# Some low parts of split operands made by adding transfers instead of VectorE subtractions

## The chip, the cores and the metric

The kernel runs on one core of a Trainium2 chip. The engines of the core have one in-order instruction stream each: TensorE (PE in the profile; its weight loads are PEld), VectorE (DVE), ScalarE (ACT), GpSimd (POOL) and SyncE (SP). SP, ACT and POOL can issue transfers (DMA). The metric is the device time of one execution in microseconds. The kernel before takes 1139.64 us, the median of three runs (1139.55 to 1140.3).

## The reference, cut to what matters

One layer of a streaming encoder on 512 tokens of width 1024, in float32:

```python
f = swiglu(rms_norm(h, ffn1_pre_g[l]), ffn1_w1[l], ffn1_w3[l], ffn1_w2[l])
h = h + 0.5 * rms_norm(f, ffn1_post_g[l])
u = rms_norm(h, mix_pre_g[l])
q, k, v, xr, xg = jnp.split(u @ w_in[l], splits, axis=-1)
xr = causal_conv(xr, conv_w[l], conv_b[l])
hr = rg_lru(xr, ...)                                   # a scan over the tokens
y_a = (hr * jax.nn.gelu(xg)) @ w_lru_out[l]
y_b = swa_sink_attention(q, k, v, attn_sinks[l], bias) @ w_attn_out[l]
g = jax.nn.sigmoid(u @ w_gate[l] + b_gate[l]).reshape(b, s, N_BRANCHES, d)
merged = g[:, :, 0] * y_a + g[:, :, 1] * y_b
h = h + rms_norm(merged @ w_o[l], mix_post_g[l])
f = swiglu(rms_norm(h, ffn2_pre_g[l]), ffn2_w1[l], ffn2_w3[l], ffn2_w2[l])
h = h + 0.5 * rms_norm(f, ffn2_post_g[l])
```

## The kernel before

**Split operands.** Every float32 operand x of a product is split into a high part (x rounded to the type `fp32r` by an ACT copy) and a low part (x minus the high part, a DVE subtraction). A product then takes three matmuls: high by high, low by high, high by low. `split2` (L192) makes both parts; weights get theirs in `split_to` (L152) or in `Pairs.prep` (L493). So each weight tile of 128x1024 (512 KB) costs one load by SP, one ACT copy (`whi`), one DVE subtraction (`wlo`) and its matmuls.

**The stages.** First FFN; its output product `tok_gemm`, which at the end leaves the normed activations transposed in `uT` (high and low part); then the mixer, around which this case turns; then the attention, the output projections and the second FFN. In the mixer PE runs in this order: the eight `xr` tiles, the eight gate tiles `wg` 0 to 7 (each a unit of 24 matmuls, `mm_feat` L197, with lines L204 to L206), the V product (L1113 to L1115, four token groups), the four pairs of `xg` tiles (`GeluPairs`, L621), then `wk`, `wq` and the attention.

**The xg pairs.** Two weight tiles (ra, rb) and two halves of the tokens are multiplied with seven instead of eight products of quarter blocks (a Strassen-Winograd scheme). On the weight side there are the sums S1 to S4 (`S12`, `S34`, made by POOL, L518 to L524), on the activation side T1 to T4 (keys `t1` to `t4` of `X3`). The seven products of pair n are groups of 12 matmuls (`mm_s`, L473 to L475), in the order a11, S1, (the a22 of pair n-1), S2, a12, S4, S3. ACT copies results between groups (L638, L640, L644, L656), because a later group goes on adding in the same bank. Step i of `prep(m, i)` makes the weights of pair m:

- i = 0: the sums S12 and S34, on POOL
- i = 1: high and low part of ra, which holds a11 and a12
- i = 2, 3: high and low part of S12 and of S34
- i = 4: high and low part of a22, a half of rb

During pair n the loop `run` calls prep(n+1, 1) after group S1, prep(n+1, 2) after S2, prep(n+1, 3) after S4, then prep(n+1, 4) and prep(n+2, 0). So the a11 of pair n+1 uses what prep(n+1, 1) made some five groups earlier, and S1 of pair n+1 what prep(n+1, 2) made. Pair 0 is prepared ahead, at the places in `PREP_AT`; `PREP_1` is the place of prep(1, 0).

**T1 to T4.** POOL makes them from copies `xf` of the transposed activations (L1066); `t_hi` copies the high part on ACT and `t_lo` subtracts on DVE. `T_AT` gives the places of both.

**What sets the order.** The text of the program is the order of each engine's instructions. `later(n, fn)` puts off work by n places, `point()` marks a place (two in each unit of 24 matmuls, one in each V group); a lower rank goes first. Instructions wait on semaphores for what they read, and for the last user of the slot which they write: all big tiles come from a pool of 42 slots, so a load by SP waits until a slot is free.

**Beside it.** The recurrent branch runs on ACT and DVE during the mixer. Its scans (L1047, a product, and L1048, the scan, eight of each, tiles `ig`) come at the last places (`SCAN_AT`), after ACT's square roots (L1044), and share DVE with the V parts (`V`, L195) and with the weights of the xg pairs.

Of the kernel before, what the change touches and what calls it, by code (L numbers as in the profile page):

```python
# [11 lines left out]
F32R = mybir.dt.float32r  # L12
AF = mybir.ActivationFunctionType
ALU = mybir.AluOpType

P = 128
SEQ = 512
D = 1024
# [33 lines left out]
def hybrid_layer(ctx: ExitStack, tc: tile.TileContext, a: dict, out: bass.AP):  # L52
    nc = tc.nc
    act, dve, pool, pe, sp = nc.scalar, nc.vector, nc.gpsimd, nc.tensor, nc.sync

    cp = ctx.enter_context(tc.tile_pool(name="cp", bufs=1))
    sm = ctx.enter_context(tc.tile_pool(name="sm", bufs=4))
    sb = ctx.enter_context(tc.tile_pool(name="sb", bufs=NSLOT))
    pp = ctx.enter_context(tc.tile_pool(name="pp", bufs=8, space=bass.MemoryType.PSUM))
# [3 lines left out]
    def slot(shape, dt=F32, name="s"):  # L63
        uid[0] += 1
        return sb.tile(shape, dt, tag="slot", name=f"{name}_{uid[0]}")
# [9 lines left out]
    def f32(ap):  # L75
        return ap.bitcast(F32)
# [25 lines left out]
    order = []  # L102
# [33 lines left out]
    raws, pairs = {}, {}  # L136
# [10 lines left out]
    def dma_to(n):  # L147
        while st["dma"] < min(n, len(order)):
            dma_one(st["dma"])
            st["dma"] += 1  # L150

    def split_to(n):  # L152
        while st["split"] < min(n, len(order)) and st["split"] not in paired:
            k = st["split"]
            dma_to(k + 1)
            r = raws.pop(k)
            hi = slot([P, D], F32R, name="whi")
            lo = slot([P, D], F32R, name="wlo")
            act.activation(hi, r, AF.Copy)
            dve.tensor_tensor(out=lo, in0=r, in1=f32(hi), op=ALU.subtract)  # L160
            pairs[k] = (hi, lo)
            st["split"] += 1

    def get(nm, i, ahead=2, rawahead=3):

        k = st["get"]
        assert order[k] == (nm, i), (order[k], nm, i)
        dma_to(k + 1 + ahead)
        split_to(k + 1 + ahead)
        dma_to(st["split"] + rawahead)  # L170
        st["get"] += 1
        return pairs.pop(k)
# [5 lines left out]
    def later(n, fn, rank=1):  # L178
        uid[0] += 1
        due.append((now[0] + n, rank, uid[0], fn))  # L180
# [11 lines left out]
    def split2(hi, lo, src):  # L192

        act.activation(hi, src, AF.Copy)  # L194
        dve.tensor_tensor(out=lo, in0=src, in1=f32(hi), op=ALU.subtract)  # L195
# [138 lines left out]
    def tok_gemm(nm, xs, n, R, gpost_name, scale, gpre_name, first, x_to=None, xf=None, spill=False, then=None, eps=None):  # L334
# [38 lines left out]
        us, trs = {}, {}  # L373
        ep = lambda t: D * EPS if eps is None else eps[:, t : t + 1]
        split_to(st["get"] + len(first))
        dma_to(st["split"] + 2)
        for t in range(NT):
# [48 lines left out]
    def get_ahead():  # L426
        split_to(st["get"] + 2)
        dma_to(st["split"] + 3)
# [49 lines left out]
    class Pairs:  # L478
# [14 lines left out]
        def prep(self, m, i, eng=None):  # L493
            if m >= len(self.jobs) or (m, i) in self.ready:
                return
            self.ready.add((m, i))
            k = self.k0 + 2 * m
            if i == 0:
                if k not in loaded or k + 1 not in loaded:
                    self.raws(m)  # L500
                s12, s34 = slot([P, 2 * QH], name="S12"), slot([P, 2 * QH], name="S34")
                self.w[m] = {"r": (raws.pop(k), raws.pop(k + 1)), "s": (s12, s34)}
            W = self.w[m]
            (ra, rb), (s12, s34) = W["r"], W["s"]
            a11, a12, a21, a22 = ra[:, :QH], ra[:, QH:], rb[:, :QH], rb[:, QH:]

            def both(src, w=2 * QH):
                hi = slot([P, w], F32R, name="whi")
                lo = slot([P, w], F32R, name="wlo")
                split2(hi, lo, src)  # L510
                return hi, lo

            def halves(p, a, b):
                W[a] = p[0][:, :QH], p[1][:, :QH]
                W[b] = p[0][:, QH:], p[1][:, QH:]

            def sums34(e):
                e.tensor_tensor(out=s34[:, QH:], in0=a12, in1=s12[:, QH:], op=ALU.subtract)  # L518
                e.tensor_tensor(out=s34[:, :QH], in0=a11, in1=a21, op=ALU.subtract)  # L519

            if i == 0:
                e = eng or pool
                e.tensor_tensor(out=s12[:, :QH], in0=a21, in1=a22, op=ALU.add)
                e.tensor_tensor(out=s12[:, QH:], in0=s12[:, :QH], in1=a11, op=ALU.subtract)  # L524
                if self.R is None:
                    sums34(e)
            elif i == 1:
                halves(both(ra), "a11", "a12")
            elif i == 2:
                if self.R is not None:  # L530
                    sums34(dve)
                halves(both(s12), "s1", "s2")
            elif i == 3:
                halves(both(s34), "s3", "s4")
            elif i == 4:
                t = slot([P, 2, QH], F32R, name="w22")
                split2(t[:, 0, :], t[:, 1, :], a22)
                W["a22"] = t[:, 0, :], t[:, 1, :]
            if all((m, x) in self.ready for x in range(5)):
                del W["r"], W["s"]  # L540
# [219 lines left out]
    xg, tg = {(hh, th): slot([P, 4, 256], name="xg") for hh in range(2) for th in range(2)}, {}  # L760
# [101 lines left out]
    def uview(hh, th):  # L862

        return lambda e, k: uT[:, e, 4 * hh + k, th * 256 : th * 256 + 256]

    def pair_view(p):
        return lambda e, k: p[e][:, k, :]
# [77 lines left out]
    for f in range(NG, NC1):  # L945
# [4 lines left out]
    bs = tok_gemm(  # L950
        "w2a", hid, FT, RF, "ffn1_post_g", 0.5, "mix_pre_g", [("xr", i) for i in range(4)], hid.to, xf=xf, spill=True, eps=veps)
    hid = None
# [100 lines left out]
    X3 = {"b11": uview(0, 0), "b21": uview(1, 0), "b22": uview(1, 1)}  # L1053
    pairs_g = GeluPairs(("xg",), 0, 8, X3)

    def t_hi(key, src):
        X3[key] = slot([P, 4, 256], F32R, name="Xh")
        act.activation(X3[key], src, AF.Copy)

    def t_lo(key, src):  # L1060
        hi, lo = X3[key], slot([P, 4, 256], F32R, name="Xl")
        dve.tensor_tensor(out=lo, in0=src, in1=f32(hi), op=ALU.subtract)
        X3[key] = pair_view((hi, lo))

    for o_, p_, q_ in (((0, 0), (0, 1), (0, 0)), ((0, 1), (1, 1), (0, 1)), ((1, 1), (1, 1), (0, 0)), ((1, 0), (1, 0), (1, 1))):
        pool.tensor_tensor(out=xf[o_], in0=xf[p_], in1=xf[q_], op=ALU.subtract)  # L1066
    for n, (key, o_) in enumerate((("t1", (0, 0)), ("t3", (0, 1)), ("t2", (1, 1)), ("t4", (1, 0)))):
        later(T_AT[0][n], lambda key=key, o_=o_: t_hi(key, xf[o_]), 3)
        later(T_AT[1][n], lambda key=key, o_=o_: t_lo(key, xf.pop(o_)), 3)
    for i, p in enumerate(PREP_AT):  # L1070
# [50 lines left out]
    X3 = pairs_g = None  # L1121
# [221 lines left out]
    X2 = pairs_b = None  # L1343
    tok_gemm("w2b", hid, FT, RF, "ffn2_post_g", 0.5, None, [], hid.to)

# [8 lines left out]
SCAN_AT = (25, 25, 25, 25, 26, 26, 26, 26)  # L1354
SCAN_LAG = (1, 1, 2, 2, 2, 2, 3, 5)

T_AT = (3, 4, 5, 6), (13, 15, 18, 20)
PREP_AT = (19, 21, 23, 24, 25)
PREP_1 = 24
NSLOT = 42  # L1360
RF = 7
RO = 6

# [58 lines left out]
```

## Time and profile before

| | |
|---|---|
| median of three runs | 1139.64 us (1139.55 to 1140.3) |
| the profiled execution | 1139.73 us, span 1137.9 us |
| PE | 1121.4 us busy, 99% of the span |
| DVE | 832.2 us, 73% |
| ACT | 617.9 us, 54% |
| POOL | 344.5 us, 30% |
| HBM | 116.50 MB read, 7.33 MB written |

Rows of the timeline read: start in us from the span's start, length in us, engine, line, operation, written tile<-read tiles, partitions x elements and type, count; in brackets the idle time of the engine before it, and what ended it. Rows of a grouping view read: line, engine, operation, tiles and shapes, count | busy us, mean ns of one | idle time before them, and what ended it. Rows of transfers read: written tile<-source, issuing queue, count, size of each, median us from issue to landing. `uT`, `Xh` and `Xl` are activations, `whi` and `wlo` weights (the page leaves out buffer numbers), `S` the weight sums, `raw_...` loaded weights.

### The profile page before, as it was taken

How to read it: one execution, taken by the hardware profiler on the slowest of the kernel's cores; microseconds unless marked ns; L12 is line 12 of the kernel's file. 1: busy time of each engine (PE TensorE's matmuls, PEld its weight loads, DVE VectorE, ACT ScalarE, POOL GpSimd, SP SyncE). 2: the span in 40 equal slices, each digit the busy share in tenths (PEclk: the TensorE clock that was granted, in tenths of full speed). 3: DMA queues.
4: the chain of work that ended last, by engine and by line, in shares of the span. 5: the costliest groups of instructions: out<-in, count | busy, mean ns of one | idle time of the engine just before them, and what ended most of it. 6: DMA issues, size and time to landing. Idle time of an engine off the chain costs nothing.

```text
span 1137.9 us, 17855 instructions
## 1 busy us (share of the span) xinstructions
PE 1121.4 (99%) x6973; PEld 1011.6 (89%) x6973; DVE 832.2 (73%) x1235; ACT 617.9 (54%) x1101; POOL 344.5 (30%) x263
## 2 busy tenths in 40 slices
PE   9999999999999999799999999999999999999997
PEld 7899999988889878798888888889999999998886
DVE  5889989796346989986678855767899777975313
ACT  7755555474236598466656653356555555574211
POOL 0043444200002302421456543000965566700000
PEclk9999999999999999899999999999999999999999
DMA  9226553365304112234133233531323332255101
GB/s 346 89 88 150 139 119 112 82 220 162 129 38 167 56 56 74 75 99 162 44 88 93 89 84 125 174 122 39 111 87 100 112 106 81 93 189 179 40 19 56
DMA packets 37139, 124.98 MB, mean 110 GB/s; under 512 B 4528, under 2 KB 6448, under 8 KB 37056
## 3 DMA queue, kind: packets, MB, share of 16 engines
q1 hardware_dynamic: 34128, 114.89, 31.0%
q0 software_dynamic: 2640, 8.43, 3.7%
q8 instruction: 55, 0.90, 0.3%
q10 hardware_dynamic: 288, 0.52, 0.1%
q14 instruction: 28, 0.23, 0.1%
HBM read 116.50 MB, written 7.33 MB: 109 GB/s over the span
## 4 chain that ended last, share of the span: by engine, by line
PE 96%; DVE 2%; ACT 0%; issue 0%; DMA 0%; DVEq 0%; SPq 0%
PE c L474 12%; PE c L473 12%; PE c L475 12%; PE f L204 10%; PE f L205 10%; PE f L206 9%; PE acc L222 8%; PE acc L223 8%; PE acc L224 8%; PE pt L1221 1%; DVE ig L1048 1%; DVE ig L1047 1%; PE s L1185 1%; PE s L1184 1%; PE tr L314 1%; PE o L1237 1%
## 5 line engine op out<-in xcount | busy, mean ns | idle before, releaser
L474 PE MATMUL c<-uT,wlo 128*128 128x256 f32 x504 | 143.3, 284 | 7.6 <-DVE wlo L195 7.6
L204 PE MATMUL f<-uT,whi 128*128 128x512 f32 (+1 forms) x408 | 146.7, 360 | 0.0
L205 PE MATMUL f<-uT,wlo 128*128 128x512 f32 (+1 forms) x408 | 145.3, 356 | 0.0
L206 PE MATMUL f<-uT,whi 128*128 128x512 f32 (+1 forms) x408 | 145.2, 356 | 0.0
L474 PE MATMUL c<-Xh,wlo 128*128 128x256 f32 x504 | 143.2, 284 | 0.0
L475 PE MATMUL c<-uT,whi 128*128 128x256 f32 x504 | 143.2, 284 | 0.0
L473 PE MATMUL c<-Xh,whi 128*128 128x256 f32 x504 | 143.1, 284 | 0.0
L473 PE MATMUL c<-uT,whi 128*128 128x256 f32 x504 | 143.0, 284 | 0.0
L475 PE MATMUL c<-Xl,whi 128*128 128x256 f32 x504 | 142.9, 284 | 0.0
L222 PE MATMUL acc<-whi,hT 128*128 128x512 f32 x352 | 137.1, 390 | 0.0
L223 PE MATMUL acc<-wlo,hT 128*128 128x512 f32 x352 | 137.0, 389 | 0.0
L224 PE MATMUL acc<-whi,hT 128*128 128x512 f32 x352 | 136.9, 389 | 0.0
L195 DVE TENSOR_TENSOR wlo<-S,whi 128x1024 fp32r<-128x1024 f32 x84 | 124.1, 1477 | 2.0 <-ACT whi L194 1.2
L474 PEld LDWEIGHTS c<-uT,wlo 128*128 128x128 f32 x504 | 97.3, 193 | 7.9 <-DVE wlo L195 7.8
L194 ACT ACTIVATE whi<-S 128x1024 fp32r<-128x1024 f32 x84 | 86.1, 1054 | 22.0 <-DVE S L519 22.0
L473 PEld LDWEIGHTS c<-Xh,whi 128*128 128x128 f32 x504 | 97.2, 193 | 0.4 <-issue 0.3
L474 PEld LDWEIGHTS c<-Xh,wlo 128*128 128x128 f32 x504 | 97.0, 192 | 0.4 <-DVE wlo L195 0.3
L475 PEld LDWEIGHTS c<-uT,whi 128*128 128x128 f32 x504 | 97.3, 193 | 0.0
L473 PEld LDWEIGHTS c<-uT,whi 128*128 128x128 f32 x504 | 97.2, 193 | 0.0
L475 PEld LDWEIGHTS c<-Xl,whi 128*128 128x128 f32 x504 | 97.0, 193 | 0.0
L204 PEld LDWEIGHTS f<-uT,whi 128*128 128x128 f32 x408 | 77.1, 189 | 12.1 <-issue 1.4
L206 PEld LDWEIGHTS f<-uT,whi 128*128 128x128 f32 x408 | 77.1, 189 | 11.0
(341 smaller groups left out, 2797.3 us busy)
## 6 DMA issues: line engine op xcount, KB each, us to landing
raw_w2a<-in_w2a_dram SPq DMA_DIRECT2D x22, 512.0 KB, 3.9
raw_w1b<-in_w1b_dram SPq DMA_DIRECT2D x22, 512.0 KB, 4.3
raw_w3b<-in_w3b_dram SPq DMA_DIRECT2D x22, 512.0 KB, 3.9
raw_w2b<-in_w2b_dram SPq DMA_DIRECT2D x22, 512.0 KB, 4.2
raw_w3a<-in_w3a_dram SPq DMA_DIRECT2D x21, 512.0 KB, 4.5
raw_w1a<-in_w1a_dram SPq DMA_DIRECT2D x20, 512.0 KB, 4.4
raw_wg<-in_wg_dram SPq DMA_DIRECT2D x16, 512.0 KB, 3.7
raw_xr<-in_xr_dram SPq DMA_DIRECT2D x8, 512.0 KB, 3.7
```

What stands on the lines that cost most here:

```text
L194: act.activation(hi, src, AF.Copy)
L195: dve.tensor_tensor(out=lo, in0=src, in1=f32(hi), op=ALU.subtract)
L204: pe.matmul(ps[:, c0:c1], wh[:, s], h_, start=k == 0, stop=False)
L205: pe.matmul(ps[:, c0:c1], wl[:, s], h_, start=False, stop=False)
L206: pe.matmul(ps[:, c0:c1], wh[:, s], l_, start=False, stop=k == KT - 1)
L222: pe.matmul(acc[n], x[:, 0, c], wh[:, s], start=first, stop=False)
L223: pe.matmul(acc[n], x[:, 0, c], wl[:, s], start=False, stop=False)
L224: pe.matmul(acc[n], x[:, 1, c], wh[:, s], start=False, stop=last)
L314: pe.transpose(ps[:, k * P : (k + 1) * P], hg[:, kk * P : (kk + 1) * P], ident)
L473: pe.matmul(ps, wh[:, s], xh, start=first, stop=False, skip_group_check=True)
L474: pe.matmul(ps, wl[:, s], xh, start=False, stop=False, skip_group_check=True)
L475: pe.matmul(ps, wh[:, s], xl, start=False, stop=k == 3, skip_group_check=True)
```

## The change

A new function makes a low part without DVE: ACT writes the negative of the high part (a copy with scale -1, rounded the same way) into the low part's slot, and a transfer issued by POOL then adds the original float32 values onto it, from where they lie (DRAM for weights, the slot for T1 to T4). Eleven low parts are made this way: T1 to T4, the gate tiles 0 to 3, and the ra of the xg pairs 1, 2 and 3 (not of pair 0). Each takes one DVE subtraction away and adds one ACT copy, one issue on POOL and 512 KB of transfer. The low parts of T1 to T4 are moved from the places 13, 15, 18, 20 to 4, 5, 6, 7, one place behind their high parts.

```diff
+    def split_dma(r, src, shape=(P, D), hi=None):
+
+        lo = slot(list(shape), F32R, name="wlo")
+        if hi is None:
+            hi = slot(list(shape), F32R, name="whi")
+            act.activation(hi, r, AF.Copy)
+        act.activation(lo, r, AF.Copy, scale=-1.0)
+        pool.dma_start(out=lo, in_=src, accum_op=ALU.add)
+        return hi, lo
...
     def split_to(n):
...
             r = raws.pop(k)
-            hi = slot([P, D], F32R, name="whi")
-            lo = slot([P, D], F32R, name="wlo")
-            act.activation(hi, r, AF.Copy)
-            dve.tensor_tensor(out=lo, in0=r, in1=f32(hi), op=ALU.subtract)
-            pairs[k] = (hi, lo)
+            if order[k] in BY_DMA:
+                nm, i = order[k]
+                pairs[k] = split_dma(r, a[nm][i * P : (i + 1) * P, :])
+            else:
+                hi = slot([P, D], F32R, name="whi")
+                lo = slot([P, D], F32R, name="wlo")
+                act.activation(hi, r, AF.Copy)
+                dve.tensor_tensor(out=lo, in0=r, in1=f32(hi), op=ALU.subtract)
+                pairs[k] = (hi, lo)
...
             elif i == 1:
-                halves(both(ra), "a11", "a12")
+                nm, t_ = order[k]
+                p = split_dma(ra, a[nm][t_ * P : (t_ + 1) * P, :]) if nm in BY_DMA and m else both(ra)
+                halves(p, "a11", "a12")
...
     def t_lo(key, src):
-        hi, lo = X3[key], slot([P, 4, 256], F32R, name="Xl")
-        dve.tensor_tensor(out=lo, in0=src, in1=f32(hi), op=ALU.subtract)
-        X3[key] = pair_view((hi, lo))
+        X3[key] = pair_view(split_dma(src, src, (P, 4, 256), X3[key]))
...
-T_AT = (3, 4, 5, 6), (13, 15, 18, 20)
+T_AT = (3, 4, 5, 6), (4, 5, 6, 7)
...
+BY_DMA = {("wg", i) for i in range(4)} | {"xg"}
```

## The prediction

> **What bounds the kernel now.** I read the page first, then the waits of TensorE, and only then the place where the one large wait stands.
>
> ```profile
> span 1137.9 us, 17855 instructions
> ...
> PE 1121.4 (99%) x6973; PEld 1011.6 (89%) x6973; DVE 832.2 (73%) x1235; ACT 617.9 (54%) x1101; POOL 344.5 (30%) x263
> ...
> PE 96%; DVE 2%; ACT 0%; issue 0%; DMA 0%; DVEq 0%; SPq 0%
> ```
> ```profile
> engine line waited for: us in total, times, longest us
> PE c L474 <- DVE wlo L195: 7.6, 1, 7.6
> ```
>
> TensorE (PE) is busy for 99% of the span, and the chain that ended last is PE but for 2% on DVE. PE's only large wait is 7.6 us, once, on a low part that DVE makes. So work taken off DVE is worth something only as far as it ends that wait sooner, and whatever makes PE wait anew costs its full length. The timeline of PE puts the wait in time; the rows are the first matmuls on either side and the starts of the groups that follow.
>
> ```profile
> 471.44 0.28 PE L473 MATMUL c<-uT,whi 128*128 128x256 f32 x1
> 479.34 0.58 PE L474 MATMUL c<-uT,wlo 128*128 128x256 f32 x1 [7.63 <-DVE wlo L195]
> ...
> 482.32 0.58 PE L474 MATMUL c<-Xh,wlo 128*128 128x256 f32 x1
> ...
> 485.78 0.39 PE L473 MATMUL c<-Xh,whi 128*128 128x256 f32 x1
> ...
> 491.76 0.28 PE L474 MATMUL c<-uT,wlo 128*128 128x256 f32 x1
> ...
> 501.84 0.28 PE L474 MATMUL c<-uT,wlo 128*128 128x256 f32 x1
> ```
>
> It is the second of the four x_gate pairs (n=1, counted from 0). At 471.44 its first matmul has the high part of a11; the second needs the low part and gets it at 479.34. At 482.32 the product with S1 waits once more, for the low part of S12. Pair 2 needs its first low part at 491.76, pair 3 at 501.84. What DVE did until then:
>
> ```profile
> 459.07 0.42 DVE L195 TENSOR_TENSOR V<-v,V 128x256 fp32r<-128x256 f32 x1 [2.18 <-ACT V L194]
> 459.41 1.83 DVE L1047 TENSOR_TENSOR ig<-xc_t,ig 128x512 f32<-128x512 f32 x1
> ...
> 462.41 0.67 DVE L1047 TENSOR_TENSOR ig<-xc_t,ig 128x512 f32<-128x512 f32 x1
> ...
> 469.30 2.20 DVE L1048 TENSOR_TENSOR_SCAN ig<-xc_t,ig 128x512 f32<-128x512 f32 x1
> ...
> 473.14 2.17 DVE L1048 TENSOR_TENSOR_SCAN ig<-xc_t,ig 128x512 f32<-128x512 f32 x1
> 475.23 1.68 DVE L1047 TENSOR_TENSOR ig<-xc_t,ig 128x512 f32<-128x512 f32 x1
> ...
> 478.09 1.20 DVE L195 TENSOR_TENSOR wlo<-raw_xg,whi 128x1024 fp32r<-128x1024 f32 x1
> 479.20 0.68 DVE L1047 TENSOR_TENSOR ig<-xc_t,ig 128x512 f32<-128x512 f32 x1
> 479.92 1.22 DVE L1048 TENSOR_TENSOR_SCAN ig<-xc_t,ig 128x512 f32<-128x512 f32 x1
> 481.06 1.20 DVE L195 TENSOR_TENSOR wlo<-S,whi 128x1024 fp32r<-128x1024 f32 x1
> ...
> 482.51 0.41 DVE L650 TENSOR_TENSOR cc<-c,ct 128x256 f32<-128x256 f32 x1
> ```
>
> From 459.07 DVE runs through the V parts and eight products and scans, then the two low parts that PE needs. The row at 459.07 decides most of this case: before it DVE had been idle for 2.18 us. It was not behind; it waited for ACT.
>
> ```profile
> 404.53 1.06 ACT L159 ACTIVATE whi<-raw_wg 128x1024 fp32r<-128x1024 f32 x1
> ...
> 409.27 1.05 ACT L159 ACTIVATE whi<-raw_wg 128x1024 fp32r<-128x1024 f32 x1
> ...
> 454.36 0.38 ACT L194 ACTIVATE V<-v 128x256 fp32r<-128x256 f32 x1 [2.09 <-PE v L1115]
> ...
> 466.16 1.05 ACT L194 ACTIVATE whi<-raw_xg 128x1024 fp32r<-128x1024 f32 x1
> ...
> 483.01 1.28 ACT L630 ACT_TABLE_LOAD   x1 [10.99 <-DVE cc L650]
> ...
> 485.36 0.37 ACT L638 ACTIVATE ct<-c 128x256 f32<-128x256 f32 x1
> ...
> 485.89 1.06 ACT L194 ACTIVATE whi<-raw_xg 128x1024 fp32r<-128x1024 f32 x1
> 486.84 0.38 ACT L666 ACTIVATE cc<-c 128x256 f32<-128x256 f32 x1
> ```
>
> ACT in turn had waited 2.09 us for PE at 454.36. So the chain into the wait is anchored to PE's own progress at 454.36, and no work removed from DVE before 459.07 moves it.
>
> **The eight low parts before the wait: 0 us.** T1 to T4 and the gate tiles 0 to 3 leave DVE (groups by line in the stretch from 372 to 515 us):
>
> ```profile
> L160 DVE TENSOR_TENSOR wlo<-raw_wg,whi 128x1024 fp32r<-128x1024 f32 x8 | 9.8, 1219 | 1.2 <-ACT whi L159 1.2
> ...
> L1062 DVE TENSOR_TENSOR Xl<-xf,Xh 128x1024 fp32r<-128x1024 f32 x4 | 6.0, 1494 | 0.0
> ...
> L982 ACT ACTIVATE xc_t<-f,vec 128x512 f32<-128x512 f32 x7 | 5.4, 778 | 13.1 <-PE f L206 13.1
> ```
>
> That is 6.0 + 4 x 1.22 = 10.9 us of DVE work, all before 459.07, and by the row there DVE only idles longer. ACT gets eight more copies of 1.05 us. Six fit into the 13.1 us for which it waits for PE's projections in this stretch (L982); the two behind 404.53 and 409.27 delay it by 2 us, which its idle 2.09 us at 454.36 covers alone. Without that cover the 2 us would enter the chain.
>
> **The first weights of pair 1: 1.1 us off the chain.** DVE loses the row at 478.09; the next starts at 479.20, so what follows is 1.11 us earlier. ACT's copy at 466.16 is followed by a second, so POOL can issue at about 468.1. PE wants that part at 471.5 but is stopped anyway at the next group until DVE has made S12's low part; only a landing later than 481 would show.
>
> **POOL's sums: 0.3 us.** The products and scans are long while POOL works.
>
> ```profile
> 455.05 1.29 POOL L523 TENSOR_TENSOR S<-raw_xg 128x512 f32<-128x512 f32 x1 [14.97 <-DVE wlo L195]
> ...
> 468.68 1.73 POOL L523 TENSOR_TENSOR S<-raw_xg 128x512 f32<-128x512 f32 x1 [7.99 <-PE c L474]
> ```
>
> 459.41 took 1.83 where 462.41 took 0.67: 1.16 us. With slots free earlier, the loads for pair 1's sums are issued earlier and those sums can start when PE is through the last gate tile, near 451 (a group of 12 such matmuls lasts (501.84 - 491.76) / 7 = 1.44 us, and the first V product has two such lengths ahead of 454.36). Then 459.41 is freed, but the same sums slow the DVE work before 459.07 and use up its 2.18 us of idleness. Ends: 0 and 1.16 us; I take 0.3, nearer the low end because the sums overlap DVE work in either place. Pair 2's sums stand on POOL behind the new issue, which waits for ACT's copy: about 469 instead of 468.68, the same scans slowed (473.14: 2.17 against 1.22 at 479.92). They do not get out of the way.
>
> Together S12's low part comes 1.4 us sooner. The cc row at 482.51, ACT's table load at 483.01 behind it and the copy at 485.36 that the group at 485.78 needs follow, so pair 2 could start at 491.76 - 1.4 = 490.4.
>
> **The first weights of pairs 2 and 3: the loss.** Here DVE was in time. The new path is: high copy, low copy, issue, landing. For pair 2 the high copy moves to 485.89 - 1.4 = 484.5; the low copy is one step (486.84 - 485.89 = 0.95) behind and ends at about 486.4. L is the time from there to the landing.
>
> ```profile
> raw_wq<-in_wq_dram SPq DMA_DIRECT2D x8, 512.0 KB, 4.1
> ...
> BT<-bias_scr POOLq DMA_DIRECT2D x16, 128.0 KB, 3.1
> bc_ffn_post_g<-in_ffn_post_g_dram POOLq DMA_DIRECT2D x2, 512.0 KB, 4.4
> ...
> raw_wk<-in_wk_dram SPq DMA_DIRECT2D x2, 512.0 KB, 3.6
> ```
>
> The trace has no adding transfer. Low end: a plain one of the same size from the same queue, 4.4 us. High end: two of them in turn, 8.8 us. Between: 384 KB more cost 4.4 - 3.1 = 1.3 us, so the moving part of 512 KB is about 1.7 us, and destination and source must both be read: 4.4 + 1.7 = 6.1. The wk loads now fall in the same microseconds; 4.1 against 3.6 us for two groups of equal loads makes that 0.4 more. I take L = 6.5 us. The Trainium skill (Collectives: The Full Stack, section "The bandwidth ceiling: the fold count and why AG ≠ RS ≠ AR") puts the cost of an add in flight in the second source read, not in the adding; by that alone L would be 6.1, and no row here can show it.
>
> Pair 2 then starts at 486.4 + 6.5 = 492.9 instead of 491.76: 1.1 us late, although the wait before it shrank. Pair 3's low part: its high copy stands behind ACT's copies of pair 2's first two groups. Two groups of 1.44 us, two short copies' 0.5 us and two long ones' 1.9 us make 5.3 us after the start; plus L it is 492.9 + 5.3 + 6.5 = 504.7 instead of 501.84: **2.9 us late**. Nothing after it is changed, and PE has no slack to the end.
>
> Sum on the profiled execution (1139.73 us: the span of 1137.9 and 1.8 around it): + 2.9 = 1142.6; on the median of 1139.64, **1142.5 us**. In general the change is 486.4 + 5.3 + 2L - 501.84 = 2L - 10.1 us while both parts are late; it is nil at L = 5.05, and +0.2% (2.3 us, about what can be told from no change) at L = 6.2.
>
> **Rivals.** *The transfer costs no more than a plain one* (not slower). Place: the landings of pairs 2 and 3; it decides below L = 5.05. With L = 4.5 pair 2 starts at 490.9 and pair 3 at 501.0, PE's own pace: -0.8 us, 1138.8. For it: the 4.4 us row. Against it: nothing shows that the second read is hidden.
>
> *Cheap transfers, and pair 2's sums leave the scans.* If POOL's sums come after DVE's scans, up to some 3.9 us more (four long rows from 469.30 to 475.23, each about 1 us over 1.22 or 0.67) leave the chain; with L = 4.5 the result is -0.8 - 3.9 = -4.7: 1135. Against it: the sums are queued right behind an issue at 468.
>
> *Slow transfers.* At L = 8.8 the formula gives +7.5. The gate tiles are then late too: tile 2's low copy ends near 406.5 and its unit starts at 415.02, so it has 8.5 us.
>
> ```profile
> 415.02 0.39 PE L204 MATMUL f<-uT,whi 128*128 128x512 f32 x1
> ```
>
> That adds up to 0.5: +8, 1147.6. For it: an addition in flight may run at a rate that no row shows.
>
> **How the numbers follow.** Forecast (L from 5.6 to 8.5, both late; its own range 1140.7 to 1146.5) 0.42, of which 0.1 lies within 0.2%; plain cost 0.26, of which 0.2 within, 0.05 faster and 0.01 slower; cheap with the sums moved 0.13, faster; slow transfers 0.19, slower. So faster 0.18, within 0.2% 0.30, slower 0.52. The range reaches to 1136.5, which leaves out most of the sums' case, and to 1149, an L of 9.5.
>
> **What would show it.** Right: PE's wait for a low part from DVE is gone at pair 1's first group and stands a group later for S12, ending near 480.9; two new waits of PE on adding transfers, at pairs 2 and 3, 2 to 3 us each; no PE wait at the gate tiles; landings of the adding transfers near 6.5 us. Wrong: landings of 5 us or less (then no new waits), landings over 8.5 (then waits at gate tiles 2 and 3 as well), a DVE chain after 459 without the long rows, or an ACT that no longer waits for PE near 454.

## The result, and the profile after

| | before | after |
|---|---|---|
| median | 1139.72 us (1139.55 to 1140.3, six runs) | 1146.1 us (1143.9 to 1147.19, six runs) |
| ratio after to before | | 1.0052 (95% interval 1.0039 to 1.0065) |
| profiled execution, its span | 1139.73 us, 1137.9 us | 1145.55 us, 1142.8 us |

The change makes the kernel 6.4 us slower; the forecast was 2.9 us slower. Three executions in the calls of the next section, of 1381, 1497 and 2250 us, are slow ones and enter no ratio. The first rows below are from the page of the kernel after: span, busy times, and the engines' shares of the chain that ended last.

```profile
span 1142.8 us, 17893 instructions
...
PE 1122.5 (98%) x6973; PEld 1012.7 (89%) x6973; DVE 823.7 (72%) x1224; ACT 628.1 (55%) x1112; POOL 353.7 (31%) x274
...
PE 55%; DMA 1%; DVE 0%; issue 0%; ACT 0%; DVEq 0%
```

DVE has 8.5 us less to do, ACT 10.2 us and POOL 9.2 us more. A DMA now stands in the chain. DVE's share can't be compared with the 2% before: the shares sum to 56%, because the view follows the chain back only to pair 3's adding transfer, issued at 498.70, and 644.1 of the 1142.8 us lie behind it. What DVE did at pair 1 comes earlier. What PE waits for after (engine, line, waited for: us in total, times, longest), and where these waits and the groups behind them stand in PE's timeline:

```profile
PE c L488 <- DMA wlo<-in_xg_dram: 8.5, 3, 4.0
PE c L488 <- DVE wlo L209: 2.8, 1, 2.8
```
```profile
475.55 0.58 PE L488 MATMUL c<-uT,wlo 128*128 128x256 f32 x1 [4.04 <-DMA wlo<-in_xg_dram]
481.23 0.58 PE L488 MATMUL c<-Xh,wlo 128*128 128x256 f32 x1 [2.76 <-DVE wlo L209]
...
485.38 0.28 PE L487 MATMUL c<-Xh,whi 128*128 128x256 f32 x1
...
493.06 0.39 PE L488 MATMUL c<-uT,wlo 128*128 128x256 f32 x1 [1.64 <-DMA wlo<-in_xg_dram]
...
506.18 0.39 PE L488 MATMUL c<-uT,wlo 128*128 128x256 f32 x1 [2.77 <-DMA wlo<-in_xg_dram]
```

The one wait of 7.6 us has become two at pair 1 (4.04 for the adding transfer, 2.76 for S12's low part), and each of pairs 2 and 3 has a new one. S12's wait ends 1.09 us sooner than before (482.32), but the next group, S2, starts only 0.40 us sooner (485.78 before). Pair 2 starts 1.30 us late, pair 3 4.34 us late ("start" of a pair is its first matmul with a low part). DVE, ACT and POOL in the same stretch:

```profile
460.07 0.68 DVE L1063 TENSOR_TENSOR ig<-xc_t,ig 128x512 f32<-128x512 f32 x1
...
461.92 0.67 DVE L1063 TENSOR_TENSOR ig<-xc_t,ig 128x512 f32<-128x512 f32 x1
...
468.81 2.73 DVE L1064 TENSOR_TENSOR_SCAN ig<-xc_t,ig 128x512 f32<-128x512 f32 x1
...
479.98 1.20 DVE L209 TENSOR_TENSOR wlo<-S,whi 128x1024 fp32r<-128x1024 f32 x1
```
```profile
454.15 0.38 ACT L208 ACTIVATE V<-v 128x256 fp32r<-128x256 f32 x1 [2.09 <-PE v L1129]
...
484.80 1.06 ACT L157 ACTIVATE whi<-raw_xg 128x1024 fp32r<-128x1024 f32 x1
485.74 1.06 ACT L158 ACTIVATE wlo<-raw_xg 128x1024 fp32r<-128x1024 f32 x1
...
497.35 1.05 ACT L158 ACTIVATE wlo<-raw_xg 128x1024 fp32r<-128x1024 f32 x1
```
```profile
451.09 1.85 POOL L537 TENSOR_TENSOR S<-raw_xg 128x512 f32<-128x512 f32 x1 [12.90 <-PE f L219]
...
468.24 0.88 POOL L159 DMA_DIRECT2D wlo<-in_xg_dram  x1 [10.45 <-ACT ct L660]
468.83 1.62 POOL L537 TENSOR_TENSOR S<-raw_xg 128x512 f32<-128x512 f32 x1
...
498.70 0.88 POOL L159 DMA_DIRECT2D wlo<-in_xg_dram  x1 [2.69 <-ACT cc L682]
```

The low part of S12 moves from 481.06 to 479.98. The copies of pairs 2 and 3 end at 486.80 and 498.40; from there to the waiting matmul it is 6.26 and 7.78 us. The transfers of the stretch from 372 to 515 us (count, size, median us from issue to landing), and then, each from a window of its own, pair 2's transfer, gate tile 3's and pair 3's with the wk load beside it (SP issues the load at 498.47, POOL the transfer at 498.70):

```profile
wlo<-in_wg_dram POOLq DMA_DIRECT2D x4, 512.0 KB, 6.8
```
```profile
wlo<-in_xg_dram POOLq DMA_DIRECT2D x1, 512.0 KB, 5.9
```
```profile
wlo<-in_wg_dram POOLq DMA_DIRECT2D x1, 512.0 KB, 7.9
```
```profile
raw_wk<-in_wk_dram SPq DMA_DIRECT2D x1, 512.0 KB, 4.0
wlo<-in_xg_dram POOLq DMA_DIRECT2D x1, 512.0 KB, 7.4
```

### The profile page after: what moved, and what is told of

It reads as the page before. It is cut to its first block, busy times and chain, and to the rows that moved or that the text cites. A ratio compares the mean times of both kernels' runs of the same rounds, so it can differ in the third digit from the quotient of the medians.

```text
span 1142.8 us, 17893 instructions
## 1 busy us (share of the span) xinstructions
PE 1122.5 (98%) x6973; PEld 1012.7 (89%) x6973; DVE 823.7 (72%) x1224; ACT 628.1 (55%) x1112; POOL 353.7 (31%) x274
## 4 chain that ended last, share of the span: by engine, by line
PE 55%; DMA 1%; DVE 0%; issue 0%; ACT 0%; DVEq 0%
PE c L488 6%; PE c L487 6%; PE c L489 6%; PE f L218 6%; PE f L220 6%; PE f L219 6%; PE acc L238 5%; PE acc L237 5%; PE acc L236 5%; PE pt L1235 1%; PE s L1199 1%; DMA wlo<-in_xg_dram 1%; PE s L1198 1%; PE o L1251 1%; PE o L1252 1%; PE tr L328 0%
## 5 line engine op out<-in xcount | busy, mean ns | idle before, releaser
L489 PE MATMUL c<-Xl,whi 128*128 128x256 f32 x456 | 129.0, 283 | 0.0
L489 PEld LDWEIGHTS c<-Xl,whi 128*128 128x128 f32 x456 | 87.5, 192 | 0.0
```

Of the source, the lines that this page charges most:

```text
L489: pe.matmul(ps, wh[:, s], xl, start=False, stop=k == 3, skip_group_check=True)
```

## The experiments

All were timed beside the kernel before on the same chip; a ratio is to the runs of before in the same call (medians of before: 1140.08 us for the runs without the pairs, with the pairs only, with copies, and with pair 1 only; 1139.87 us for the late wk load, the earlier issue, the spare matmuls with pair 1 only, and S12 without them; 1140.06 us for the other four).

**Which part loses.** The pairs back on DVE:

```diff
-BY_DMA = {("wg", i) for i in range(4)} | {"xg"}
+BY_DMA = {("wg", i) for i in range(4)}
```

> The changed kernel with the low parts of the x_gate pairs 1, 2 and 3 back on VectorE; T1 to T4 and the gate tiles 0 to 3 are still made by adding transfers. Theory (the loss sits in the adding transfers of pairs 2 and 3 alone): within 0.2% of the kernel before, about 1139.7 us; TensorE again stops about 7.6 us at the first group of pair 1, and at nothing else that belongs to an x_gate pair. Rival (the eight early transfers cost something themselves, through ScalarE or through memory traffic): 1141 to 1146 us. Second rival (they are worth something, because GpSimd's sums and VectorE's chain start sooner): 1137 to 1138.5 us.

Measured: 1140.65 us, ratio 1.0005 (0.9996 to 1.0014), runs from 1139.94 to 1141.77. In the profile PE waits 7.3 us at pair 1 again. The eight early transfers gain nothing; their cost is 0.6 us in the median, and the interval holds zero.

The opposite: T1 to T4 and the gate tiles on DVE, only the pairs by adding transfers.

```diff
-        X3[key] = pair_view(split_dma(src, src, (P, 4, 256), X3[key]))
+        hi, lo = X3[key], slot([P, 4, 256], F32R, name="Xl")
+        dve.tensor_tensor(out=lo, in0=src, in1=f32(hi), op=ALU.subtract)
+        X3[key] = pair_view((hi, lo))
...
-T_AT = (3, 4, 5, 6), (4, 5, 6, 7)
+T_AT = (3, 4, 5, 6), (13, 15, 18, 20)
...
-BY_DMA = {("wg", i) for i in range(4)} | {"xg"}
+BY_DMA = {"xg"}
```

> The changed kernel with T1 to T4 and the gate tiles back on VectorE, T1 to T4 at their old places; only the first weights of the x_gate pairs 1, 2 and 3 are made by adding transfers. Theory (the loss sits in pairs 2 and 3): as the changed kernel, 1144 to 1147 us, with waits of TensorE on adding transfers at pairs 2 and 3 of 1.5 to 3 us each. Rival (the early transfers bring part of the loss): 1141 to 1143 us.

Measured: 1145.32 us, ratio 1.0048 (1.0035 to 1.006), with waits of 1.68 and 2.91 us at pairs 2 and 3. So 5.2 us of the loss belong to the pairs.

**What makes the landings late.** The transfers of pairs 2 and 3 copy instead of adding:

```diff
-        pool.dma_start(out=lo, in_=src, accum_op=ALU.add)
+        if plain:
+            pool.dma_start(out=lo, in_=src)
+        else:
+            pool.dma_start(out=lo, in_=src, accum_op=ALU.add)
```

> The changed kernel, but the transfers of pairs 2 and 3 copy instead of adding; the low part of these two weights is then the weight itself, so the subtraction of the high part is left out there. Theory (the reading of the destination is what makes the landing late): landings near 4.5 us, waits of TensorE at pairs 2 and 3 gone or under 0.7 us, 1138.5 to 1140 us. Rival (ScalarE's second copy, GpSimd's issue and the loads of wk beside them make it late): landings of 5.5 us or more and 1142 to 1146 us.

Measured: 1140.64 us, ratio 1.0006 (0.9998 to 1.0015). Pair 2's and pair 3's transfers in this kernel, from two windows of the transfers' view:

```profile
wlo<-in_xg_dram POOLq DMA_DIRECT2D x1, 512.0 KB, 3.9
```
```profile
wlo<-in_xg_dram POOLq DMA_DIRECT2D x1, 512.0 KB, 4.7
```

Same size, queue and source: 3.9 and 4.7 us instead of 5.9 and 7.4. The waits at pairs 2 and 3 are gone (pair 3's first low-part matmul starts at 501.99, 0.28 us behind the one ahead of it where 0.12 is the step). Adding costs 2.0 and 2.7 us a landing, and without it PE does not wait there.

Next, the wk load beside pair 3's transfer. Both are issued right behind the same event, the end of ACT's copy at 498.40: POOL waits for it, and the copy reads the raw tile, whose slot a later load can take (SP's waits after show 9.7 us for this copy, once). (The 0.1 us of the text below is to the end of SP's issue.) Here its load is asked for a pair later:

```diff
-                self.raws(n + 3)
+                if n != 2:
+                    self.raws(n + 3)
```

> The changed kernel, with the load of the second wk tile, which in the changed kernel is issued within 0.1 us of pair 3's adding transfer, asked for a pair later. Theory (the difference between pair 2's landing of 5.9 us and pair 3's of 7.4 us is this load beside it): pair 3's adding transfer lands in about 6 us, its wait shrinks by about 1.4 us, and the time is about 1144.7 us. Rival (pair 3's landing is long for another reason): 7.4 us again and 1146 us.

Measured: 1142.96 us, ratio 1.0025 (1.0015 to 1.0035). Pair 3's transfer and its wait:

```profile
wlo<-in_xg_dram POOLq DMA_DIRECT2D x1, 512.0 KB, 5.5
```
```profile
504.02 0.39 PE L488 MATMUL c<-uT,wlo 128*128 128x256 f32 x1 [0.80 <-DMA wlo<-in_xg_dram]
```

The landing fell from 7.4 to 5.5 us, more than expected, and the wait from 2.77 to 0.80. So beside the adding transfer the one plain load costs 1.9 us. Others fit, though no run isolates them: in the kernel after, pair 1's transfer took 7.3 us with a load issued 0.30 us behind it, and gate tile 3's 7.9 us with one 0.27 us ahead, while pair 2's took 5.9 us with the load 1.24 us behind. Pair 3 starts 2.16 us sooner than after; the medians lie 3.1 us apart, and the rest is not in the rows of the pairs.

If lateness is all, an earlier issue cures it:

```diff
                 self.prep(n + 1, 3)
+                self.prep(n + 2, 1)
```

(with the raw tiles of a pair taken over at whichever step of `prep` comes first)

> The changed kernel, but the copies and adding transfers of the first weights of pairs 2 and 3 are issued a pair earlier (right behind the S34 parts of the pair before). Theory (the whole loss is the lateness of these two landings): TensorE's waits on adding transfers at pairs 2 and 3 vanish and the time falls to 1139 to 1141 us, as with these two low parts on VectorE. Rival (the extra traffic and copies cost something wherever they stand): it stays above 1142 us.

Measured: 1139.32 us, ratio 0.9994 (0.9985 to 1.0003). No wait at pairs 2 and 3 is left; all eleven adding transfers are still made. The whole loss of the pairs was lateness, and the whole change then brings nothing that can be told from no change.

**Where the gain at pair 1 went.** Only pair 1's first weights by an adding transfer:

```diff
-                p = split_dma(ra, a[nm][t_ * P : (t_ + 1) * P, :]) if nm in BY_DMA and m else both(ra)
+                p = split_dma(ra, a[nm][t_ * P : (t_ + 1) * P, :]) if nm in BY_DMA and m == 1 else both(ra)
```

(with T1 to T4 and the gate tiles on DVE as above)

> Only pair 1's first weights are made by an adding transfer; all other low parts are VectorE subtractions as before. Theory (one 1.1 us subtraction leaves VectorE's chain into the wait): 1.0 to 1.5 us faster than before, about 1138.4 us; the wait of TensorE at pair 1 moves one group later and ends 1.1 us sooner, pairs 2 and 3 start without a wait. Rival (the chain is set by something else): 1139.7 us.

Measured: 1141.26 us, ratio 1.0008 (1.0000 to 1.0017): no gain, if anything a loss. DVE's chain did gain: S12's low part starts at 480.38 instead of 481.06. That is 0.68, not 1.11, because DVE's products and scans beside POOL's sums end with these sums, and the sums now stand behind an issue of 0.96 us at 468.56. These are the first and the last of pair 2's sums, and the scan beside the first, in this kernel:

```profile
469.20 1.65 POOL L537 TENSOR_TENSOR S<-raw_xg 128x512 f32<-128x512 f32 x1
...
474.62 2.19 POOL L533 TENSOR_TENSOR S<-raw_xg,raw_xg 128x512 f32<-128x512 f32 x1
```
```profile
469.23 2.71 DVE L1064 TENSOR_TENSOR_SCAN ig<-xc_t,ig 128x512 f32<-128x512 f32 x1
```

The scan ends 1.09 us behind the first sum (471.94 and 470.85), as before (471.50 and 470.41), although it starts 0.03 us behind the sum's start here and 0.62 us before. The last sum ends at 476.81 instead of 476.37, which is the 0.4 us that is missing.

And PE does not use the rest: S2 starts at 485.80, as before. (The profiled execution, 1140.19 us, is the second fastest of the eleven; what makes the median 1.1 us longer is not in its rows.) The clock shows why S2 is not sooner. PE's busy time and the granted clock in stretches of 3.4 us, cut where the clock changes (from:to, length, PE busy and its instructions, clock, share of the DMA engines, GB/s), of before and then of this kernel:

```profile
470.00:473.40 3.40, 1.72 (x15) 1.00 0.28 46
473.40:476.80 3.40, 0.00 (x0) 1.00 0.46 135
476.80:480.20 3.40, 0.86 (x4) 0.50 0.37 130
480.20:483.60 3.40, 3.35 (x16) 0.50 0.00 0
```
```profile
470.90:474.30 3.40, 0.91 (x8) 1.00 0.95 223
474.30:477.70 3.40, 1.93 (x9) 0.51 0.63 202
477.70:481.10 3.40, 1.00 (x5) 0.50 0.00 0
481.10:484.60 3.50, 2.97 (x14) 0.50 0.00 0
```

The clock is halved behind a stretch in which PE was busy for 0.00 or 0.91 us (not behind 1.72), and stays halved behind 0.86, 1.93 and 1.00. Before, the long stop leaves 6.8 us of half clock; here, with the stop cut in two, no stretch is busy enough until the last, and it is 10.2 us. The Trainium skill (TensorE: Matmul & The Clock Gate, section "What's actually happening") tells of a free-running window of 3413 ns; the trace agrees, 6.8 and 10.2 us being two and three of them.

To test it, spare matmuls keep PE busy through both stops (the code ahead of the a11 group; the same ahead of S1):

```diff
+                if n == 1:
+                    for _ in range(30):
+                        pe.matmul(bu, W["a11"][0][:, :P], X["b11"](0, 0), start=True, stop=False, skip_group_check=True)
                 mm_s(W["a11"], X["b11"], bu)
```

> As the run with pair 1 only, with 30 spare matmuls ahead of each of the two groups at which TensorE stops in pair 1 (they write the bank that the group's first real matmul overwrites; no result is changed). Theory (the two shorter stops leave TensorE at half its clock for 10.2 us where the one long stop left 6.8 us, and that eats the 1.1 us that VectorE's chain gained): the granted clock stays at 1.00 from 471 to 486 us, group S2 of pair 1 starts about 485.1 instead of 485.8, the spread of the runs shrinks, and the median is 1139 to 1139.6 us against 1141.26 with pair 1 only. Rival (the clock has no part in it; group S2 waits for ScalarE anyway): as pair 1 only, 1140 to 1142.5 us, or more if the spare matmuls themselves delay the groups.

Measured: 1139.43 us, ratio 0.9996 (0.9986 to 1.0005), against 1.0008 (1.0000 to 1.0017) for the same kernel without them; the intervals touch, so the rows below carry the argument. The clock, and the start of S2:

```profile
471.60:486.00 14.40, 12.95 (x103) 1.00 0.33 91
```
```profile
485.19 0.39 PE L487 MATMUL c<-Xh,whi 128*128 128x256 f32 x1 [0.44 <-ACT ct L657]
```

The clock holds, the runs spread over 0.8 instead of 2.6 us, and S2 now waits for ACT's copy ct, 0.6 us sooner than before. That copy is the next bound.

The same in the kernel before (58 and 8 spare matmuls), where the copy ct ends at 485.73 and so hides the half clock:

> The kernel before with 58 spare matmuls in its one long stop at pair 1 (and 8 ahead of the next group). Theory (in the kernel before the half clock is hidden: ScalarE's copy ct ends at 485.7, so S2 of pair 1 cannot start before that at any clock): the clock stays at 1.00 and the time stays within 0.3 us of before, 1139.6 to 1140.2 us. Rival (half clock costs the kernel before 3.4 us of halved work, 1.5 to 3.4 us of time): 1136.5 to 1138.5 us.

Measured: 1139.82 us, ratio 1.0000 (0.9991 to 1.0008), clock 1.00 from 471.5 to 486. S2 starts at

```profile
485.72 0.39 PE L473 MATMUL c<-Xh,whi 128*128 128x256 f32 x1 [0.44 <-ACT ct L641]
```

instead of 485.78. The half clock cost the kernel before nothing that the interval shows, as the theory said. In the kernel after (30 spare matmuls at each stop):

> The changed kernel with 30 spare matmuls ahead of each of the two groups at which TensorE stops in pair 1. Theory (half clock takes back what the shorter chain gained, the adding transfers of pairs 2 and 3 bring the rest): the clock stays at 1.00 through pair 1, S2 starts 0.5 to 0.7 us sooner, and the time is 1 to 1.7 us less, 1144.4 to 1145.1 us; the waits at pairs 2 and 3 stay. Rival (the clock has no part in the changed kernel's loss): 1146 us.

Measured: 1145.82 us, ratio 1.0054 (1.004 to 1.0068): a miss. The clock held, and from the start of pair 1's a11 to S2 it took 13.54 us (472.52 to 486.06) instead of 14.15 (471.23 to 485.38), 0.6 less, as expected. But pair 2 waits for its adding transfer anyway, and this hangs on ACT's copies at 484.80 and 485.74, which hang on DVE and not on PE's clock: its wait grew from 1.64 to 1.91 us. I had not asked what hides the gain. The profiled execution also shows a wait that the other profiles do not have:

```profile
PE f L219 <- DMA wlo<-in_wg_dram: 0.9, 1, 0.9
```

Gate tile 3's transfer took 9.2 us here. After, it took 7.9 us from an issue at 412.29, and the first matmul that reads this low part starts at 420.48, so it was in time by 0.3 us.

**A version that beats both.** S12 of pair 1 by an adding transfer too (pairs 2 and 3, T and gates on DVE):

```diff
-                halves(both(s12), "s1", "s2")
+                p = split_dma(s12, s12) if "xg" in self.jobs[m] and m == 1 else both(s12)
+                halves(p, "s1", "s2")
```

> As the run with pair 1 only (T1 to T4, gate tiles, pairs 2 and 3 on VectorE), and the low part of pair 1's S12 is made by an adding transfer as well. Theory (the wait for S12 is a wait for VectorE alone): the second stop of TensorE, 2.9 us, shrinks to under 1 us or goes, VectorE's sums cc and ScalarE's table load behind them come 1.1 us sooner, and the time falls by 1 to 2 us below the run with pair 1 only, to about 1139 us. Rival (the transfer lands as late as VectorE was, beside the first one): no gain, 1140 to 1142 us.

Measured: 1137.32 us, ratio 0.9981 (0.9972 to 0.999), better than expected. S12's transfer lands in 8.9 us, just when the group wants it (wait 0.6 us). Of the ten runs in the ratio, six lie between 1136.9 and 1137.3, four between 1138.7 and 1139.4; the profiled one is of the four. Its clock, in the last two stretches of half clock:

```profile
477.50:480.90 3.40, 2.81 (x14) 0.50 0.47 105
480.90:484.30 3.40, 3.40 (x17) 0.50 0.02 5
```

With 2.81 us busy the clock stayed halved; in the run with plain copies 2.93 us brought it back:

```profile
475.75:479.15 3.40, 2.93 (x12) 0.50 0.19 78
479.15:482.55 3.40, 1.02 (x8) 1.00 0.00 0
```

One more stretch at half clock with PE busy costs 1.7 us, the distance of the two groups of runs. The six have no profile, but each run's mean granted clock is on record: 0.996 or 0.997 for the six, 0.994 or 0.995 for the four. One stretch of 3.4 us at half clock is 0.0015 of the span, so one stretch less fits. With spare matmuls (30 and 14):

> The run with pair 1's first weights and S12 by adding transfers, with spare matmuls ahead of the two groups that wait for them (30 and 14; they write what the first real matmul overwrites). Theory (with VectorE's chain 1.1 us shorter still, half clock is what sets group S2 of pair 1): the clock stays at 1.00, S2 starts near 483 instead of 484.5, where ScalarE's copy ct sets it, and the time is 1135.5 to 1136.2 us, faster than both kernels. Rival (S2 waits for the S12 transfer itself): 1137 us, as without the spare matmuls.

Measured: 1137.09 us, ratio 0.9974 (0.9964 to 0.9984), eight runs within 0.8 us. S2 starts where expected, at

```profile
482.76 0.38 PE L487 MATMUL c<-Xh,whi 128*128 128x256 f32 x1
```

and the profiled execution is 1.9 us below the one without spare matmuls (1137.02 against 1138.94). The median gains only 0.2 us: most runs without them were among the six, so the expected 1135.5 to 1136.2 was reckoned from the wrong run. This median is the lowest of the study, though the interval overlaps with that of the kernel without spare matmuls.

Last, no adding transfer at all: the kernel before with its last two scans put off.

```diff
-SCAN_LAG = (1, 1, 2, 2, 2, 2, 3, 5)
+SCAN_LAG = (1, 1, 2, 2, 2, 2, 20, 22)
```

> The kernel before, without any adding transfer; only the last two products and scans of the recurrent branch, which pair 3 alone needs, are put off to pairs 2 and 3. Theory (the wait at pair 1 is a matter of VectorE's order: these four rows, 4.8 us, stand ahead of the low parts): the a11 low part comes 2.9 us sooner and that of S12 4.8 us sooner, group S2 of pair 1 starts at 482 to 483 instead of 485.8, and the time is 1136 to 1137 us. Rival (VectorE, fully busy from 490 to 502 us, pays the same later, as a wait of TensorE for pair 3's low parts): 1139 to 1141 us.

Measured: 1138.28 us, ratio 0.9983 (0.9974 to 0.9991), 1.3 us short of the expected 1137. S2 starts at 484.35 instead of 482 to 483: the low part of a11 now runs beside POOL's sums and takes 2.21 us instead of 1.20, and PE works at half clock from 476.5 to 483.3. No wait appeared at pair 3. So the order of DVE's work alone brings 0.17%, of the 0.26% that the best kernel with adding transfers reached.

## Why the prediction was right, and what was off

The forecast (slower, through late adding transfers at pairs 2 and 3) was right in place and mechanism: the waits named for pairs 1, 2 and 3 all appeared (pair 2's, 1.64 us, is shorter than the 2 to 3 us named), and earlier issues or plain copies remove the loss. The size was short: 1142.5 against 1146.1 us, 3.6 us too low, inside the range.

*The eight early low parts, 0 us.* Nothing gained, as said: ACT still waits 2.09 us for PE at 454.15. That they cost nothing holds within the interval of the first experiment, but its cover is thinner than I wrote. I showed the room for gate tile 2; the tight one is tile 3, whose landing of 7.9 us leaves 0.3 us, and which with 9.2 us made PE wait 0.9 us in one profile.

*Pair 1's first weights, -1.1, and POOL's sums, -0.3.* Both sums started as forecast (451.09 and 468.83), and the scan chain from 459 on was 0.49 us sooner (462.41 to 461.92). What failed is the 0.3: no head start on DVE gets past pair 2's sums, because the scan beside the first of them ends 1.09 us behind that sum whenever it starts (471.50 and 470.41 before, 471.54 and 470.45 after), and the products and scans beside the other three end with theirs. The last sum ends at 476.41 instead of 476.37. So S12's low part came 1.08 instead of 1.4 us sooner: the 1.11 of the subtraction, less what POOL is late. I carried the gain straight on to PE; alone it does not reach PE's end (1.0008), because half clock eats it. In the kernel after it reaches pair 2 through ACT's copies, which the forecast used. Pair 1's own adding transfer landed 7.60 us behind its copy (467.95 to 475.55) instead of 6.5, inside the room that the forecast gave it (until 481), but it is what PE's first stop at pair 1 now waits for.

*Pairs 2 and 3: the term that was mis-sized.* The low copy of pair 2 ended at 486.80 (486.4 forecast), from the start of pair 2 to the end of pair 3's low copy it was 5.34 us (5.3), and L was 6.26 and 7.78 us where I took 6.5 for both. In the general formula the change at pair 3 is 0.4 - 0.24 + 0.04 + 1.28 = 1.5 us more than the forecast (2.9, or 2.86 before rounding), so 4.3, which is what the timeline shows. The addition itself was sized well: in the same place it lands 1.8 to 2.0 us later than a copy (5.7 and 5.9 against 3.9), where I had put 1.7 for the second read, and the Trainium skill (Collectives: The Full Stack, "The bandwidth ceiling: the fold count and why AG ≠ RS ≠ AR") has that read as the cost too; no run here separates the read from the addition, so the agreement is in size only. What failed is the 0.4 us for the wk loads: 1.9 us, because the load starts within 0.3 us of the transfer. With the load put off, L at pair 3 was 5.79 us (498.23 to 504.02), against the 6.1 forecast without it. I had read the 0.4 off two groups of plain loads, which say nothing of an adding transfer with a load starting beside it.

*The other 2.1 us.* Of the profiled execution's 5.8 us, 4.3 are at pair 3, 0.6 between there and the span's end and 0.9 outside the span (2.75 against 1.83 us); the median lies 0.6 above the profiled execution. None of these was isolated. Landings near their limit (gate tile 3) can move runs by up to 0.9 us. That they make the spread of 3.3 us after is not shown: before spread over 0.75 us beside it, but over 1.8 to 3.6 us in the calls of the experiments.

*The rivals.* Plain cost: refuted for the adding transfer, and shown with the copies, where the time is 1140.64 and not 1138.8, since the gain at pair 1 is lost. Sums out of the scans: they did not move. Slow transfers, L = 8.8: not reached at the pairs; at gate tile 3 one profile has a landing of 9.2 us.

## What to carry to other kernels

Price a new transfer by what starts in the same microsecond: freeing a buffer and issuing the transfer are often the same event, and the next load then runs beside it. Moving work to a slower path is free only as far ahead as its latency reaches; here an issue one pair earlier turned +6.4 us into no change. A head start on one engine counts only up to the next place where its work ends with another engine's, as DVE's scans do with POOL's sums here. And a wait that is cut in two can cost as much as the whole one, if TensorE's clock stays down longer, so look at the granted clock behind a stop before a shorter wait is booked as a gain.

## What was not expected of the hardware

- An adding transfer of 512 KB landed in 5.5 us with no load starting beside it, in 7.4 us with one, in 7.9 and once 9.2 us at gate tile 3; T4's, issued behind another adding transfer, took 9.1 us after and 10.3 us with the earlier issue. A copy from the same queue landed in 3.9 and 4.7 us. The issue of an adding transfer holds POOL for 0.86 to 0.98 us, that of a plain one for 0.57 and 0.59.
- The granted clock goes by stretches of 3.4 us: halved behind one with PE busy 1.1 us or less (not behind 1.72), full again behind 2.93 us or more (not behind 2.81). In the kernel with the earlier issue a stop of 2.52 us was enough to halve it (0.98 us busy from 471.45 to 474.85), and where the stretches lie differs from run to run.
- Scans and products of DVE beside POOL's sums of pair 2 end 1.07 to 1.09 and 0.54 to 0.56 us behind the sum, whenever they started, in the kernels before and after and in seven of the experiments. (A product that starts ahead of the first sum, at 468.58 of before, is not held.) POOL's issue itself did not slow DVE: with S12 by transfer, a scan at 469.34 beside the issue at 468.53 (0.98 us) took 1.23 us.
